# Feed-forward products of a two-block network in 2x2 blocks, with seven products in place of eight

## The chip, the cores and the metric

The kernel runs on one core of a Trainium2 chip. The metric is the device time of one launch in microseconds (us). Every engine of the core works through its own queue of instructions: TensorE (PE) for matrix products, VectorE (DVE), ScalarE (ACT) and GpSimd (POOL) for what is done to their results, and the queue of SyncE (SP) for transfers.

## The reference

A sequence of 512 tokens with 1024 features goes through two blocks, all in float32. The first has two layers, the second one. Each layer is a mixer (attention of several kinds, or RWKV, S5 and gated linear attention), an attention over a memory, and a feed-forward part, so that there are three feed-forward parts. Their inner width is 2816, which is 22 tiles of 128 features. Those of the first block (layers 0 and 1) and of the second are:

```python
def swiglu(h, w_gate_up, w_down):
    g, u = jnp.split(h @ w_gate_up, 2, axis=-1)
    return (jax.nn.silu(g) * u) @ w_down

def conv_ffn(h, w_up, conv_w, conv_b, w_down):
    u = h @ w_up
    u = lax.conv_general_dilated(u, ...) + conv_b      # over 3 tokens, per feature
    gate, val = jnp.split(u, 2, axis=-1)
    return (jax.nn.silu(gate) * val) @ w_down
```

`h` is the RMS norm of `x`, and the result is added to `x`.

## The kernel before

Features lie on the partitions and the 512 tokens along them, so that `x` is eight tiles of 128x512. Float32 values are multiplied as two float32r parts, a high part (ACT, `split` L246 or L310) and a low part, the value less its high part (DVE, `lo` L243, or L312 for weights). `mm3` (L276 to 282) makes three matrix products of each pair: high by high, high by low, low by high. The product of both low parts is left out.

Weights come through `load_split` (L306): a transfer of a chunk of 128x512 to `wraw` (7 buffers), then `wh` and `wl` (5 buffers each). `proj_g` (L316) takes a tile of 128 output features at a time, accumulates over the input tiles in one bank of PSUM of 128x512, and calls `emit` on the bank. Its moving operand is always the whole 512 tokens.

A feed-forward part (`First.ffn` L1166, `Second.ffn` L2342) has two halves of 11 inner tiles. In each, the up stage makes a gate tile and a value tile per inner tile (48 matrix products with eight input tiles). DVE takes the gate out of PSUM times 1/rms, ACT applies the silu, POOL scales once more by 1/rms (L1180), DVE multiplies with the value tile and the result is split. The down stage then makes eight output tiles from these 11 (33 products each), and DVE adds each to `x` (L671). After the second half's sums, `normed` splits `x` times the next gain, and POOL adds up the squares (L446). The second block's part has the convolution on DVE and ACT in the place of the silu's simple chain.

Other work is woven in: jobs are generators, and `fill(us)` runs about so many microseconds of them. In the second feed-forward part one job is there, `s5_make_g`, which computes the tables of S5 on DVE and POOL (L1947 to L2031). Scratch tiles come from pools by stream, which `room` sizes (`z` and a letter). The order of instructions on each engine is set when the program is built, by a list scheduler of the tile framework which goes by the order of the program, by what is ready in its own account of time, and by free buffers. At run time each engine keeps to that order.

Of the kernel before, what the change touches and what calls it, by code (L numbers as in the profile page):

```python
# [10 lines left out]
F32 = mybir.dt.float32  # L11
F32R = mybir.dt.float32r
AF = mybir.ActivationFunctionType
ALU = mybir.AluOpType
# [10 lines left out]
KEEP = {"x": 8, "xs": 16, "acc": 2}  # L25
NRAW = 7
NW = 5
# [14 lines left out]
def chunked(w, cw):  # L42
    """[K, M] -> [M/cw, 128, K/128, cw]: one contiguous run per partition and chunk."""
    k, m = w.shape
    return np.ascontiguousarray(w.reshape(k // 128, 128, m // cw, cw).transpose(2, 1, 0, 3))


def tiled(w, n=2):
    """[K, M] -> [M/(128 n), n, 128, K/128, 128]: groups of n tiles of features."""
    c = chunked(w, 128)  # L50
    return c.reshape(-1, n, *c.shape[1:])


def col(v):
# [15 lines left out]
def rope_tables(ang):  # L70
    """cos, and sin with the sign of the first half, [2 * dim/2, tokens]."""
# [45 lines left out]
def layouts(x, mem, g_mix, w_in_ab, g_qa, g_ka, sink_b, w_out_ab, w_in_cd, g_cq, g_ckv, w_uq, w_ukv,  # L117
# [27 lines left out]
    o["w_gu"] = np.stack([tiled(w.reshape(D, 2 * FF)) for w in gu])  # L145
    o["w_dn"] = np.stack([np.stack([tiled(w_down[i][h * FF // 2 : (h + 1) * FF // 2], 1) for h in range(2)]) for i in range(2)])
# [9 lines left out]
class Kit:  # L156
    """The pools, the constants and the steps that the parts share."""
# [24 lines left out]
    def load(self, name, tag=None, src=None):  # L182
        """An input [128, n], for good (under a tag of its own) or as scratch."""
# [27 lines left out]
    def share(self, roles):  # L211
        """Where the roles take their banks: in turns from each of some pools."""
# [10 lines left out]
    def f(self, n=S, dt=F32, stream=None):  # L223
        """Scratch of [128, n] float32."""
        self.n += 1
        tag = self.streams[self.stream if stream is None else stream]
        return self.z.tile([128, S], dt, tag=tag, name=f"z{tag}_{self.n}", bufs=self.sizes[tag])[:, :n]

    def r(self, n=S, stream=None):
        """Scratch of [128, n] float32r."""  # L230
        return self.f(n, F32R, stream)

    def keep(self, tag, dt=F32):
        """A tile that outlives its part of the program."""
        return self.t([128, S], tag, KEEP[tag], dt)

    def u(self, n=S, stream=None):
        """A split tile [128, n]: two float32r parts."""
        return self.r(n, stream), self.r(n, stream)

# [8 lines left out]
    def split_heads(self, src, tiles, c=None):  # L249
        """The parts of four heads a tile, each head's high beside its low part, for values."""  # L250
# [8 lines left out]
    def split_scaled(self, src, c, hi, lo):  # L259
        """The parts of src times a value per partition."""  # L260
# [4 lines left out]
    def weights(self, src, keep=False):  # L265
        """A chunk [128, kt, cw] of weights from DRAM, split: the parts [128, cw] by kt."""
# [9 lines left out]
    def mm3(self, out, a, b, start, stop, **kw):  # L276
        """out += a.T @ b of split operands; the product of both low parts is below float32's last bit."""
# [6 lines left out]
    def tiles(self, w, step):  # L284
        """The parts of weights by tile of features: of split chunks, or from DRAM, [tiles, 128, kt, m]."""
# [16 lines left out]
    def by(self, *engines):  # L302
        """The engines that take, in turns, the weights' low parts."""
# [11 lines left out]
    def proj_g(self, w, xs, emit, step=128):  # L315
        """Features on partitions: out[i] = W[:, tile i].T @ x."""  # L316
# [9 lines left out]

    def proj_late(self, groups, last):
        """Products of several groups (weights, operands but the last, emit), which wait for it, last(),
        only at their end: three groups of 256 features at a time."""
# [17 lines left out]
    def proj_tok_g(self, w, xs, blocks, emit):  # L347
        """Tokens on partitions: out[b] = x[:, block b].T @ W."""
# [46 lines left out]
    def fill(self, us, own=1.0):  # L395
        """About us microseconds of jobs, in their order as far as they are ready."""
# [15 lines left out]
    def ended(self, O, t):  # L412
        """O[t], once the job that leaves it there has ended."""
# [2071 lines left out]
```

## Time and profile before

| what | us |
|---|---|
| median of 3 runs | 2789.03 (2788.32 to 2790.2) |
| span of the profiled execution | 2782.0 |
| PE, DVE, ACT, POOL busy in it | 2675.9, 1599.8, 1186.2, 517.4 |
| first feed-forward part | about 345 to 704 |
| second feed-forward part | about 1072 to 1470 |
| third feed-forward part | about 2368 to 2740 |

The span is from the first to the last instruction of the profiled execution. The runs are timed from outside, without a profile, and lie 7 us above it. Matrix products are pipelined and their ends are modelled, so their pace is read from one start to the next.

### The profile page before, as it was taken

How to read it: one execution, taken by the hardware profiler on the slowest of the kernel's cores; microseconds unless marked ns; L12 is line 12 of the kernel's file. 1: busy time of each engine (PE TensorE's matmuls, PEld its weight loads, DVE VectorE, ACT ScalarE, POOL GpSimd, SP SyncE). 2: the span in 40 equal slices, each digit the busy share in tenths (PEclk: the TensorE clock that was granted, in tenths of full speed). 3: DMA queues.
4: the chain of work that ended last, by engine and by line, in shares of the span. 5: the costliest groups of instructions: out<-in, count | busy, mean ns of one | idle time of the engine just before them, and what ended most of it. 6: DMA issues, size and time to landing. Idle time of an engine off the chain costs nothing.

```text
span 2782.0 us, 37160 instructions
## 1 busy us (share of the span) xinstructions
PE 2675.9 (96%) x13432; PEld 2152.4 (77%) x13432; DVE 1599.8 (58%) x3076; ACT 1186.2 (43%) x2208; POOL 517.4 (19%) x439
## 2 busy tenths in 40 slices
PE   8999999999999999899999889899999999999998
PEld 6668878888776787678887777687878788888886
DVE  4676654344357967973445567535443556675673
ACT  4566543233345765332334331425223445543442
POOL 5224121011211131250112331112131300100001
PEclk8999999999999999999999989699999999999999
DMA  4112223323322131333433344312211433233332
GB/s 151 35 42 77 72 84 93 101 95 95 110 78 74 49 103 56 109 121 114 142 96 131 113 163 116 99 61 62 81 54 61 124 117 102 83 96 95 99 95 68
DMA packets 172520, 258.51 MB, mean 93 GB/s; under 512 B 42528, under 2 KB 60832, under 8 KB 172320
## 3 DMA queue, kind: packets, MB, share of 16 engines
q1 hardware_dynamic: 172336, 256.13, 29.7%
q8 instruction: 106, 1.74, 0.3%
q14 instruction: 78, 0.64, 0.1%
HBM read 234.04 MB, written 22.15 MB: 92 GB/s over the span
## 4 chain that ended last, share of the span: by engine, by line
PE 54%; DVE 6%; issue 6%; POOL 2%; ACT 1%; DMA 0%; SPq 0%; POOLq 0%; DVEq 0%; ACTq 0%
PE ps_mm L280 14%; PE ps_mm L282 14%; PE ps_mm L281 14%; PE ps_ch L591 1%; DVE wl L312 1%; PE ps_si L2128 1%; POOL rs L466 1%; PE ps_tr L620 1%; PE ps_ch L1537 1%; PE ps_si L2124 0%; PE ps_si L607 0%; PE ps_ch L1610 0%; PE ps_ch L508 0%; PE ps_ch L1611 0%; PE ps_ch L1468 0%
## 5 line engine op out<-in xcount | busy, mean ns | idle before, releaser
L310 ACT CAST wh<-wraw 128x512 fp32r<-128x512 f32 (+1 forms) x777 | 474.5, 614 | 935.4 <-PE ps_mm L281 657.1
L312 DVE TENSOR_TENSOR wl<-wraw,wh 128x512 fp32r<-128x512 f32 (+1 forms) x691 | 484.3, 704 | 359.3 <-ACT wh L310 350.1
L280 PE MATMUL ps_mm<-xs,wh 128*128 128x512 f32 x1544 | 624.2, 404 | 6.2 <-ACT wh L310 5.7
L282 PE MATMUL ps_mm<-xs,wl 128*128 128x512 f32 x1544 | 612.8, 397 | 8.2 <-DVE wl L312 6.7
L281 PE MATMUL ps_mm<-xs,wh 128*128 128x512 f32 x1544 | 614.1, 398 | 0.5 <-DVE xs L262 0.3
L280 PEld LDWEIGHTS ps_mm<-xs,wh 128*128 128x128 f32 x1544 | 293.9, 190 | 77.0 <-issue 9.1
L282 PEld LDWEIGHTS ps_mm<-xs,wl 128*128 128x128 f32 x1544 | 293.7, 190 | 75.9 <-DVE wl L312 8.5
L281 PEld LDWEIGHTS ps_mm<-xs,wh 128*128 128x128 f32 x1544 | 293.8, 190 | 63.3 <-DVE xs L262 4.5
L446 POOL TENSOR_TENSOR acc<-acc,za 128x512 f32<-128x512 f32 x59 | 82.2, 1393 | 732.1 <-ACT za L442 730.4
L280 PE MATMUL ps_mm<-za,wh 128*128 128x512 f32 x460 | 183.5, 399 | 5.6 <-ACT za L246 5.0
L282 PE MATMUL ps_mm<-za,wl 128*128 128x512 f32 x460 | 182.7, 398 | 1.3 <-DVE wl L312 1.3
L281 PE MATMUL ps_mm<-za,wh 128*128 128x512 f32 x460 | 181.3, 394 | 0.1
L312 POOL TENSOR_TENSOR wl<-wraw,wh 128x512 fp32r<-128x512 f32 x86 | 113.4, 1327 | 345.5 <-ACT wh L310 283.8
L1180 POOL TENSOR_TENSOR za<-za,za 128x512 f32<-128x512 f32 x44 | 58.3, 1325 | 508.5 <-ACT za L1179 508.5
L280 PEld LDWEIGHTS ps_mm<-za,wh 128*128 128x128 f32 x460 | 87.9, 191 | 25.0 <-ACT za L246 6.2
L282 PEld LDWEIGHTS ps_mm<-za,wl 128*128 128x128 f32 x460 | 87.8, 191 | 22.0 <-DVE wl L312 1.8
L280 PE MATMUL ps_mm<-zb,wh 128*128 128x512 f32 (+1 forms) x284 | 100.3, 353 | 4.6 <-ACT zb L246 4.1
L281 PEld LDWEIGHTS ps_mm<-za,wh 128*128 128x128 f32 x460 | 87.7, 191 | 20.7 <-DVE za L243 1.0
L281 PE MATMUL ps_mm<-zb,wh 128*128 128x512 f32 (+1 forms) x284 | 98.6, 347 | 0.0
L243 DVE TENSOR_TENSOR za<-ps_tr,za 128x512 fp32r<-128x512 f32 (+3 forms) x152 | 84.3, 558 | 24.6 <-ACT za L246 23.5
L282 PE MATMUL ps_mm<-zb,wl 128*128 128x512 f32 (+1 forms) x284 | 98.3, 346 | 0.0
L466 POOL TENSOR_TENSOR rs<-sm,neghalf 128x4 f32<-128x4 f32 (+2 forms) x32 | 44.8, 1399 | 279.4 <-DVE sm L465 273.0
(592 smaller groups left out, 5013.3 us busy)
## 6 DMA issues: line engine op xcount, KB each, us to landing
wraw<-w_gu SPq DMA_DIRECT2D x176, 256.0 KB, 2.6
wraw<-w_dn SPq DMA_DIRECT2D x96, 256.0 KB, 2.6
wraw<-w_up SPq DMA_DIRECT2D x88, 256.0 KB, 2.6
wraw<-w_gate SPq DMA_DIRECT2D x48, 256.0 KB, 2.6
wraw<-w_dn SPq DMA_DIRECT2D x48, 192.0 KB, 2.3
dram<-za SPq DMA_DIRECT2D x26, 256.0 KB, 2.2
zc<-dram SPq DMA_DIRECT2D x26, 256.0 KB, 5.0
wraw<-w_cd SPq DMA_DIRECT2D x24, 256.0 KB, 2.6
```

What stands on the lines that cost most here:

```text
L243: self.nc.vector.tensor_tensor(lo, src, hi.bitcast(F32), op=ALU.subtract)
L280: mm(out, ah, bh, start=start, stop=False, **kw)
L281: mm(out, ah, bl, start=False, stop=False, **kw)
L282: mm(out, al, bh, start=False, stop=stop, **kw)
L310: self.nc.scalar.copy(hl[0], raw)
L312: eng.tensor_tensor(hl[1], raw, hl[0].bitcast(F32), op=ALU.subtract)
L446: self.nc.gpsimd.tensor_tensor(self.acc[0], self.acc[0], sq, op=ALU.add)
L466: self.nc.gpsimd.tensor_tensor(r, ms, self.neghalf[:, :n], op=ALU.pow)
L591: self.kit.nc.tensor.matmul(p, a[:, b * 128 : b * 128 + 128], c[:, k0:k1], start=i == 0, stop=i == len(self.qk) - 1)
L620: kit.nc.tensor.transpose(tr[:, i * 128 : i * 128 + 128], self.e[b][:, c : c + n], kit.ident)
L1180: nc.gpsimd.tensor_tensor(a, a, st["rb"], op=ALU.mult)
L1537: mm(p[:, i * 256 : i * 256 + 256], blk(st["ka"], e, 2 * g + i), st["ar"][2 * g + i][rows_], start=True, stop=True)
```

## The change

Two output tiles and an even number of input tiles are taken as 2x2 blocks: the weights as a11, a12, a21, a22 (output tile by even or odd input tiles), the moving operand as b11, b12, b21, b22 (even or odd input tiles by the first or last 256 tokens). The eight products of blocks become seven, after Strassen in Winograd's form. `blocks` loads the four chunks of weights, makes four sums of them on POOL and splits seven operands. `forms` makes of two moving tiles the four differences (POOL, or DVE for the last pair) and splits them. `seven` makes the products with 256 moving columns, in banks `x`, `y`, `z`, and continues to accumulate in `x` and `z` after `take` has read them.

This is used for all three down stages (`seven_added`, where each of seven results is added to a half of an `x` tile by DVE) and for the up stage of the first feed-forward part (`up_seven`). The up stages of the second and third keep `proj_g`. The inner tiles are taken in three parts of 4, 4 and 3 pairs in place of two halves of 11 tiles, and one more inner tile is made up before each down stage. The fill after each inner tile is 3.0 for 1.5 us. Memory is divided anew: `wraw` 9 buffers, weights 6, a pool `xt` of 12 tiles that forms, attention's parts and S5's jobs share, 28 tiles `m` for forms of the inner tiles, 5 tiles `s` for sums; the scratch of the mixers is smaller. The diff's other lines take away comments and docstrings.

```diff
-NRAW = 7
-NW = 5
+KEEP = {"x": 8, "xs": 16, "xt": 12, "acc": 2}
+NRAW = 9
+NW = 6
+L, R = slice(0, S // 2), slice(S // 2, S)
+PARTS = 4, 4, 3
...
+    def forms(self, f0, f1, tiles, eng=None):
+        nc = self.nc
+        sub = (eng or nc.gpsimd).tensor_tensor
+        ta, tb = self.f(), self.f()
+        sub(ta[:, L], f0[:, R], f0[:, L], op=ALU.subtract)
+        sub(ta[:, R], f1[:, R], f0[:, R], op=ALU.subtract)
+        sub(tb[:, L], f1[:, R], ta[:, L], op=ALU.subtract)
+        sub(tb[:, R], f1[:, L], tb[:, L], op=ALU.subtract)
+        one = next(tiles)
+        out = {"b11": (one[:, L], one[:, R])}
+        self.split(f0[:, L], *out["b11"])
+        for z, a, b in ((f1, "b21", "b22"), (ta, "t1", "t3"), (tb, "t2", "t4")):
+            hl = next(tiles), next(tiles)
+            self.split(z, *hl)
+            out[a], out[b] = ([y[:, h] for y in hl] for h in (L, R))
+        return out
...
+    def blocks(self, w):
...
+        def both(z):
+            hl = [self.t([128, CW], t, NW, F32R)[:, : n * 128] for t in ("wh", "wl")]
+            self.split(z, *hl)
+            return hl
+        def sum_(x, y, op):
+            z = self.f(n * 128, tag="s")
+            nc.gpsimd.tensor_tensor(z, x, y, op=op)
+            return z
+        yield both(a11)
+        yield both(a12)
+        s1 = sum_(a21, a22, ALU.add)
+        s2 = sum_(s1, a11, ALU.subtract)
+        yield both(s2)
+        yield both(s1)
+        yield both(sum_(a11, a21, ALU.subtract))
+        yield both(sum_(a12, s2, ALU.subtract))
+        yield both(a22)
+    def seven(self, w, xf, take):
...
+        x = self.bank()[:, L]
+        product(x, "b11", True)
+        take("p1", x)
...
+        y = self.bank()[:, L]
+        product(y, "b21", True)
+        take("p2", y)
...
+        product(x, "t2", False)
+        take("u2", x)
...
+        z = self.bank()[:, L]
+        product(z, "t1", True)
+        take("p5", z)
...
+        product(x, "t3", False)
+        take("u3", x)
...
+        product(z, "b22", False)
+        take("p35", z)
...
+        product(x, "t4", False)
+        take("c21", x)
+    def seven_added(self, w, xf, first, second):
+        to = dict(p1=(first, L), p2=(first, L), u2=(first, R), p5=(second, R), u3=(second, R), p35=(first, R), c21=(second, L))
+        def take(step, p):
+            z, h = to[step]
+            self.nc.vector.tensor_tensor(z[:, h], p, z[:, h], op=ALU.add)
+        return self.seven(w, xf, take)
...
+        for at, n in parts:
+            end = min(at + 2 * n + 1, 2 * tiles)
+            while c < end:
+                self.run(up(c, mid(c == 2 * tiles - 1)))
+                self.fill(3.0)
+                c += 1
+            i = parts.index((at, n))
+            for m in range(DT // 2):
+                self.run(self.seven_added(w_dn[i][m], pairs[at // 2 : at // 2 + n], x[2 * m], x[2 * m + 1]))
+                if i == len(parts) - 1:
+                    left(2 * m)
+                    left(2 * m + 1)
...
+            def take(step, p):
+                if step in ("p1", "u2", "p5"):
+                    z = {"p1": a[:, L], "u2": a[:, R], "p5": u[:, R]}[step]
+                    nc.scalar.copy(z, p)
+                elif step in ("p2", "u3", "p35"):
+                    z = {"p2": a[:, L], "u3": u[:, R], "p35": a[:, R]}[step]
+                    nc.vector.tensor_tensor(z, p, z, op=ALU.add)
+                if step == "p35":
+                    nc.vector.tensor_tensor(a, a, rb(), op=ALU.mult)
+                    act(a)
+                    nc.vector.tensor_tensor(u[:, R], u[:, R], a[:, R], op=ALU.mult)
+                elif step == "c21":
+                    nc.vector.tensor_tensor(u[:, L], p, a[:, L], op=ALU.mult)
+                    mid(u)
...
-    kit.room("aaaa", a=50)
+    kit.room("aaaa", a=12, m=28, s=5)
     f.ffn(0, f.g_mix[1])
...
-    kit.room("abbb", a=31, b=50-31)
+    kit.room("axxx", a=12, m=28, s=5)
...
     f.ffn(1, take)
```

The memory attention before the first feed-forward part gives its result through `add_forms`, which makes the forms of `x` times the gain in place of a split.

## Rows read from the trace of the kernel before

**Rows 1.** The page: span, and busy time and count of each engine.
```profile
span 2782.0 us, 37160 instructions
...
PE 2675.9 (96%) x13432; PEld 2152.4 (77%) x13432; DVE 1599.8 (58%) x3076; ACT 1186.2 (43%) x2208; POOL 517.4 (19%) x439
```
**Rows 2.** Windows: length, busy PE, PEld, DVE, ACT, POOL; clock, DMA share, GB/s.
```profile
461.00:523.00 62.00, 62.00 (x273) 51.07 (x272) 23.34 (x37) 18.02 (x30) 3.88 (x3) 1.00 0.33 93
523.00:640.00 117.00, 117.00 (x516) 96.65 (x515) 47.57 (x72) 36.82 (x61) 10.33 (x8) 1.00 0.31 98
...
1072.00:1470.00 398.00, 376.72 (x1749) 307.09 (x1748) 235.13 (x602) 140.87 (x238) 92.66 (x107) 0.97 0.35 111
2368.00:2740.00 372.00, 371.39 (x1649) 306.00 (x1648) 240.04 (x356) 170.02 (x262) 13.53 (x10) 1.00 0.31 94
```
**Rows 3.** Timeline in the first up stage: start us, duration us, instruction.
```profile
457.39 0.39 PE L282 MATMUL ps_ch<-xs,wl 128*128 128x512 f32 x1
...
457.62 0.39 PE L280 MATMUL ps_ch<-xs,wh 128*128 128x512 f32 x1
```
**Rows 4.** Timeline, products of 256 columns in the second block's memory attention.
```profile
2239.51 0.28 PE L280 MATMUL ps_mm<-zb,wh 128*128 128x256 f32 x1
2239.51 0.19 PEld L281 LDWEIGHTS ps_mm<-zb,wh 128*128 128x128 f32 x1
...
2239.98 0.28 PE L281 MATMUL ps_mm<-zb,wh 128*128 128x256 f32 x1
```
**Rows 5.** Groups by form: count, busy us, mean ns, idle before.
```profile
L312 DVE TENSOR_TENSOR wl<-wraw,wh 128x512 fp32r<-128x512 f32 x108 | 74.3, 688 | 91.2 <-ACT wh L310 91.1
L310 ACT CAST wh<-wraw 128x512 fp32r<-128x512 f32 x108 | 67.3, 623 | 178.3 <-PE ps_ch L281 60.6 <-PE ps_mm L281 59.3 <-PE ps_si L281 56.6
L1180 POOL TENSOR_TENSOR za<-za,za 128x512 f32<-128x512 f32 x22 | 28.4, 1292 | 262.8 <-ACT za L1179 262.8
...
L2246 POOL TENSOR_TENSOR zb<-zb,zb 128x256 f32<-128x256 f32 x7 | 5.6, 804 | 6.0 <-ACT zb L2245 6.0
```
**Rows 6.** Timeline of POOL and DVE where DVE starts second.
```profile
160.73 1.30 POOL L312 TENSOR_TENSOR wl<-wraw,wh 128x512 fp32r<-128x512 f32 x1 [5.36 <-ACT wh L310]
161.21 1.37 DVE L243 TENSOR_TENSOR zb<-zb,zb 128x512 fp32r<-128x512 f32 x1 [1.01 <-ACT zb L246]
```
**Rows 7.** Timeline of DVE and POOL where POOL starts second.
```profile
994.60 0.69 DVE L312 TENSOR_TENSOR wl<-wraw,wh 128x512 fp32r<-128x512 f32 x1
994.86 1.58 POOL L312 TENSOR_TENSOR wl<-wraw,wh 128x512 fp32r<-128x512 f32 x1 [2.38 <-ACT wh L310]
995.59 0.42 DVE L1083 TENSOR_TENSOR zb<-ps_mm,zb 128x256 f32<-128x256 f32 x1 [0.29 <-PE ps_mm L282]
```
**Rows 8.** Timeline of POOL and DVE near 1250 us.
```profile
1249.31 4.94 POOL L1975 TENSOR_TENSOR zb<-zb,zb 128x144 f32<-128x144 f32 x1 [2.59 <-DVE zb L1978]
...
1250.69 2.82 DVE L312 TENSOR_TENSOR wl<-wraw,wh 128x512 fp32r<-128x512 f32 x5
```
**Rows 9.** Timeline of POOL and DVE, alternating, in S5's job.
```profile
1242.09 0.50 POOL L1975 TENSOR_TENSOR zb<-zb,zb 128x144 f32<-128x144 f32 x1
1242.21 0.54 DVE L1972 TENSOR_TENSOR zb<-zb,zb 128x144 f32<-128x144 f32 x1
1242.56 0.50 POOL L1977 TENSOR_TENSOR zb<-zb,zb 128x144 f32<-128x144 f32 x1
```
**Rows 10.** Timeline at the first part's start: a low part, and who waits for it.
```profile
367.17 1.76 DVE L312 TENSOR_TENSOR wl<-wraw,wh 128x512 fp32r<-128x512 f32 x1
...
368.98 0.50 PE L282 MATMUL ps_mm<-xs,wl 128*128 128x512 f32 x1 [2.87 <-DVE wl L312]
```
**Rows 11.** Timeline of PE in the second part, where S5's job comes.
```profile
1180.65 1.94 PE L2029 MATMUL ps_ch<-ident,zb 128*128 128x128 f32 x8 [11.42 <-DVE zb L2022]
...
1183.24 0.63 PE L282 MATMUL ps_mm<-xs,wl 128*128 128x512 f32 x1
1183.67 0.63 PE L280 MATMUL ps_mm<-xs,wh 128*128 128x512 f32 x1
```

More of the change, by code (lines that the diff above doesn't have):

```diff
@@ L51, in tiled, with halved, parted, parts_of @@
     return c.reshape(-1, n, *c.shape[1:])
+def halved(w):
+    t = w.reshape(w.shape[0] // 128, 128, -1)
+    return np.concatenate([t[0::2], t[1::2]]).reshape(w.shape)
+def parted(w):
+    out, at = [], 0
+    for n in PARTS:
+        out.append(tiled(halved(w[at * 256 : (at + n) * 256])).reshape(-1))
+        at += n
+    return np.concatenate(out)
+def parts_of(src):
+    out, at = [], 0
+    for n in PARTS:
+        size = D * n * 256
+        out.append(src[at : at + size].rearrange("(c j p k m) -> c j p k m", j=2, p=128, k=2 * n, m=128))
+        at += size
+    return out
 def col(v):
@@ new lines, in blocks @@
+    def blocks(self, w):
+        nc, n = self.nc, w.shape[2] // 2
+        raw = {}
+        for j in range(2):
+            for h in range(2):
+                z = raw[j, h] = self.t([128, CW], "wraw", NRAW)[:, : n * 128]
+                nc.sync.dma_start(z.rearrange("p (k m) -> p k m", m=128), w[j, :, h * n : h * n + n, :])
+        (a11, a12, a21, a22) = raw[0, 0], raw[0, 1], raw[1, 0], raw[1, 1]
+        def both(z):
[15 more added lines that the diff above has]
+        yield both(a22)
@@ new lines, in seven, with product @@
+    def seven(self, w, xf, take):
+        a = self.blocks(w)
+        def product(p, form, start):
+            hl = next(a)
+            for k, x in enumerate(xf):
+                self.mm3(p, [z[:, k * 128 : k * 128 + 128] for z in hl], x[form], start and k == 0, k == len(xf) - 1, skip_group_check=True)
+        us = len(xf) * 0.35
+        x = self.bank()[:, L]
+        product(x, "b11", True)
+        take("p1", x)
+        yield us
+        y = self.bank()[:, L]
+        product(y, "b21", True)
+        take("p2", y)
+        yield us
+        product(x, "t2", False)
+        take("u2", x)
+        yield us
+        z = self.bank()[:, L]
+        product(z, "t1", True)
+        take("p5", z)
+        yield us
+        product(x, "t3", False)
+        take("u3", x)
+        yield us
+        product(z, "b22", False)
+        take("p35", z)
+        yield us
+        product(x, "t4", False)
+        take("c21", x)
+        yield 0
@@ L423, in flush, with ffn_parts, mid, f @@
             self.fill(1.0)
+    def ffn_parts(self, up, w_dn, x, left):
+        parts, tiles, mids = [], sum(PARTS), []
+        for n in PARTS:
+            parts.append((2 * sum(PARTS[: len(parts)]), n))
+        pairs = []
+        held = (self.f(S, F32R, tag="m") for _ in range(7 * tiles))
+        def mid(last):
+            def f(z):
+                mids.append(z)
+                if len(mids) % 2 == 0:
+                    pairs.append(self.forms(*mids[-2:], held, self.nc.vector if last else None))
+            return f
+        c = 0
+        for at, n in parts:
[10 more added lines that the diff above has]
+                    left(2 * m + 1)
     def normed(self, m, x, g, squares=True):
@@ L436, in normed, with normed_forms @@
             self.squares(m, x)
+    def normed_forms(self, m, x, g):
+        f = self.f()
+        self.nc.scalar.activation(f, x, AF.Copy, scale=g)
+        if m == 0:
+            self.xs, self.held = [], chain((self.keep("xs", F32R) for _ in range(16)), (self.keep("xt", F32R) for _ in range(12)))
+        if m % 2:
+            self.xs.append(self.forms(self.even, f, self.held, self.nc.vector if m == DT - 1 else None))
+        else:
+            self.even = f
+        self.squares(m, x)
     def squares(self, m, x, direct=1):
@@ L685, in rotate, with parts @@
         return a
-    def parts(self, a):
-        hl = self.kit.u()
+    def parts(self, a, held=True):
+        hl = [self.kit.keep("xt", F32R) for _ in range(2)] if held else self.kit.u()
         self.kit.split(a, *hl)
@@ L1169, in ffn, with rb @@
         st = {}
-        for half in range(2):
-            mid = []
-            for c in range(FT // 2):
-                def gate(j, p):
-                    if "rb" not in st:
-                        st["rb"] = kit.spread(kit.rstd(), 4)
-                    if j == 0:
-                        a = kit.f()
-                        nc.vector.tensor_tensor(a, p, st["rb"], op=ALU.mult)
-                        nc.scalar.activation(a, a, AF.Silu)
-                        nc.gpsimd.tensor_tensor(a, a, st["rb"], op=ALU.mult)
-                        st["a"] = a
-                    else:
-                        nc.vector.tensor_tensor(st["a"], p, st["a"], op=ALU.mult)
-                        hl = kit.u()
-                        kit.split(st["a"], *hl)
-                        mid.append(hl)
-                kit.run(kit.proj_g(I["w_gu"][i, half * (FT // 2) + c], xs, gate))
-                kit.fill(1.5)
-            for m in range(DT):
-                kit.run(kit.proj_g(I["w_dn"][i, half, m], mid, lambda j, p: self.down(m, p, g if half else None)))
+        def rb():
+            if "rb" not in st:
+                st["rb"] = kit.spread(kit.rstd(), 4)
+            return st["rb"]
```

95 lines of the change are left out of this document (55 added, 40 removed).

## The prediction

> **What bounds the kernel now.** I read the page first: its span is 2782.0 us, in which PE is busy 96%, DVE 58%, ACT 43% and POOL 19% [rows 1]. PE is the bound on average, but the change lies in three stages only, so the windows come next. In the first feed-forward part, in a down stage (461 to 523 us) and an up stage (523 to 640), PE is busy for the whole stretch at full clock; DVE has some 40% of each and POOL less than a tenth [rows 2]. The second loses 21 us of 398 and the third almost none [rows 2].
>
> A busy PE is not PE at its peak, so the pace is read from starts. Products of 512 columns start 0.227 us apart, 457.39 and 457.62 for two of the first up stage [rows 3]. The 273 products between 461 and 523 us come to the same: 62/273 = 0.227 us [rows 2]. One part has 22 x 2 x 8 x 3 = 1056 products up and 8 x 22 x 3 = 528 down, at 0.2275 us 240.2 and 120.1 us. These stages are bound by PE alone, and only here are fewer products worth their time.
>
> Is a product of 256 columns worth half? The memory attention has such products with weights of 128x128: of five in a row the first starts at 2239.51 and the last at 2239.98, a weight load beside each [rows 4]. Four steps in 0.47 us are 0.117 us.
>
> **PE's part.** Two tiles of output features against 2n tiles of inner ones needed 12n products of 512 columns and now need 7 x 3n = 21n of 256. With n = 4 that is 10.92 us before and 84 x 0.117 = 9.83 us after; with n = 3 it is 8.19 and 7.37 us. The first part's up stage has 22 sets with n = 4: 216.2 us for 240.2, a gain of 24.0. Each down stage has eight sets of n = 4 and four of n = 3: 108.1 for 120.1, a gain of 12.0, three times. PE gains 60 us at most. That holds where the other engines keep pace with 9.83 us a set.
>
> **What the others must do for it.** A set took four splits of weights (ACT for the high part, DVE for the low) and now takes seven, and POOL makes four sums of 128x512 besides. Prices from [rows 5]: a cast 0.62 us, a low part on DVE 0.69, a POOL operation of 128x512 1.29 and of 128x256 0.80. An ACT copy out of PSUM of half the width I count as a cast, 0.62 at most. A PSUM operation of 128x256 on DVE takes 0.42 [rows 7].
>
> Up stage with seven products, per set: ACT 7 x 0.62 + 3 x 0.62 + 0.62 for the silu + half of 3.5 casts = 7.9 us. POOL: four sums and the gate's scale, 5 x 1.29, and half of four 256-column differences, 1.6, together 8.05. DVE: seven low parts, one product of 512 and one of 256, half of 3.5 low parts for the forms, all with both inputs in SBUF, 7 x 0.69 + 0.69 + 0.42 + 1.2 = 7.1; and four operations out of PSUM, 1.7. One by one each is below 9.83. The question is whether DVE and POOL can do it at the same time.
>
> The trace says no. At 160.73 POOL begins 1.30 us of work; at 161.21 DVE begins a low part that takes 0.69 elsewhere, and it ends 0.55 us after POOL does, 1.37 us long [rows 6]. The other way: POOL begins at 994.86 under a DVE low part, and ends 1.15 us after it [rows 7]. Five low parts in a row held a small POOL operation for 4.94 us [rows 8]. DVE's operations out of PSUM do not suffer: the one at 995.59 takes 0.42 us and is over 0.43 us before POOL's end [rows 7]. So where both inputs are in SBUF, DVE and POOL take turns, and I count 0.55 us for a DVE turn of 512 columns and 1.15 for POOL's. Where operations of 144 columns alternate, POOL's start 0.47 us apart with DVE's between them, though the two records are 0.50 and 0.54 us long [rows 9]: a record holds some waiting, and a turn is shorter. And PE does wait for it: at 368.98 it has lost 2.87 us to a low part that took 1.76 us [rows 10].
>
> Turns in an up set: POOL 5 x 1.15 + 2 x 0.6 (half of 1.15, and a little) = 6.95; DVE 9.5 x 0.55 + 1.5 x 0.29 = 5.66. That is 12.6 us where PE needs 9.83 and took 10.92 before. Whole records added, without overlap, give 8.05 + 7.1 = 15.1. The Trainium skill, "SBUF — State Buffer", section "SBUF: two separate sides", states it as a rule: a DVE operation with two SBUF inputs and a GpSimd operation lock the same port pair for a whole instruction, and the other blocks; the trace agrees in kind, and by whole instructions the set would take 15.1 us, where the alternating operations show part of the start hidden [rows 9]. I take 13.8, midway, since the queues are in order: DVE stands at an accumulation that PE has not finished, or at a low part whose sum POOL has not made. 22 x 13.8 = 304 us for 240: **+63** (12.6 gives +37, 15.1 gives +92).
>
> **Down sets.** With n = 4 the turns are 4 x 1.15 + 7 x 0.55 = 8.45, under 9.83. But DVE also takes seven PSUM sums of 0.42, in order between the low parts, and four of the seven products continue in a bank whose last value must first be read, with one product of 1.4 us between. Bounds: 9.83 if everything hides; 7 x 0.69 + 7 x 0.42 + 4 x 1.29 = 12.93 if nothing does. I take 10.5, near PE's own figure since about half of the sums can lie under POOL's turns: 24 sets x (10.5 - 10.92) = **-10** (-26 to +48). With n = 3, three quarters of POOL's record are 0.97 and of a low part's 0.52, so the bounds are 7.37 and 7 x 0.52 + 7 x 0.42 + 4 x 0.97 = 10.46; I take 8.5: 12 x 0.3 = **+4** (-10 to +27).
>
> **The smaller edits.** In each last set the next norm comes too: two low parts scaled on DVE and two POOL sums of squares (four at the handover, two and no low parts at the end), which slack hid before: 3.5, 5.8 and 2.3 us of turns per set, 47 us in all over 12 sets if none is hidden, 0 if POOL may run late. **+12**, a quarter, because sums of squares can trail into the next stage. At the first part's start, eight tiles are made into forms: three pairs with 12 differences of 0.80 on POOL beside the squares, where the 2.87 us wait is today. PE's first product needs only the undiffered quarter, so I take **+8** (3 to 15). The last pair of each part is made on DVE: four dependent operations of 0.42 and a split of 1.3, about 3 us, less the products that don't need it: **+6** for three (3 to 12). The S5 job lies in the second part; PE waited 11.42 us for it until 1180.65 [rows 11]. It now gets twice the fill and 12 buffers that it shares, and POOL's and DVE's new work is in its way: **+5** (-10 to +20). The rest (nine raw buffers, six of weights, smaller rooms for attention, weights laid out in another order at equal bytes) I cost at nothing: weight transfers land in stretches where DMA is busy a third of the time [rows 2], and attention takes its keys and queries from a pool of its own for what it gives up; without that cover it would cost a few us, inside the range.
>
> **Sum.** 63 - 10 + 4 + 12 + 8 + 6 + 5 = +88. The profiled execution had a span of 2782; the median of the runs is 2789.0, 7 us around it. 2782 + 88 + 7 = **2877 us**. All lower bounds together give -3 (2786), all upper ones +261 (3050).
>
> **Rivals.**
> 1. *PE stays the bound.* POOL's sums run far enough ahead and the turns fall into gaps: every set takes PE's time, -60, and with the start and the last pairs about 2743. For it: DVE is idle more than half of the time in these stages today and POOL most of it [rows 2], and each alone stays under 9.83 us. Against it: the turns seen [rows 6 to 8], 12.6 us of them a set. It decides if a set's turns stay under 9.83 us, that is, if POOL's turn of 512 columns were 0.69 us instead of 1.15. Chance 0.13, faster.
> 2. *All at the lower bounds*: 12.6 us per up set, down sets at PE's pace, 2786. Chance 0.09, split evenly between faster, same and slower.
> 3. *The down sets are bound by the turns too*: the sums out of PSUM don't fit under POOL's turns and PE waits at each bank it continues in. 24 x 1.3 + 12 x 1.8 = +53 in place of -6, with the last sets' 30: about 2955, at most 3050. Chance 0.15.
> 4. *The clock falls.* If PE waits a quarter of the up stage, its granted clock may drop as it did after the 11 us wait, where products of 512 columns went from 0.23 to 0.43 us apart [rows 11]. A product of 256 would take half of that, a set 84 x 0.215 = 18 us, the stage 397: +157, with the rest about 2970. Against it: the waits here are of a few us at most, and the second part, which lost 21 us to its waits, kept a mean clock of 0.97 [rows 2]. Chance 0.05.
>
> The forecast keeps 0.58, with a range of its own of 2835 to 2930. "Same" means within 0.2%, 5.6 us, about what a measurement of this kernel can tell from no change. Faster 0.13 + 0.03 = 0.16, same 0.03, slower 0.58 + 0.15 + 0.05 + 0.03 = 0.81. The range that leaves out rival 1 and the upper part of rival 3, 0.2 together, is 2775 to 2980.
>
> **What would show it.** Products of 256 columns 0.117 us apart within a product set; the first up stage about 300 us long, with PE waiting before low parts of weights and DVE's low parts at a mean of 1 us or more; POOL busy for over half of that stage; down sets near 10.5 and 8.5 us. The prediction is wrong if low parts stay at 0.69 us beside a busy POOL, if PE shows no waits for them, or if 256-column products start further apart than 0.12 us.

## The result and the profile after

The changed kernel takes 2935.6 us (median of 4 runs, 2934.4 to 2936.4) for 2788.7 (4 runs of the kernel before on the same chip): 1.053 times the time before, 95% interval 1.052 to 1.055. The forecast was 2877 us with 2775 to 2980 around it, so the sign and the range hold; the size is 59 us short, and the time is just above the forecast's own range of 2835 to 2930.

The page of the changed kernel, the lines that answer to [rows 1], and the costliest groups on DVE and POOL that the change made:

```profile
span 2933.4 us, 42837 instructions
...
PE 2694.5 (92%) x15412; PEld 2246.8 (77%) x15412; DVE 2041.2 (70%) x3632; ACT 1325.0 (45%) x2531; POOL 964.8 (33%) x803
...
L272 DVE TENSOR_TENSOR wl<-zs,wh 128x512 fp32r<-128x512 f32 (+1 forms) x232 | 237.6, 1029 | 25.5 <-ACT wh L275 21.8
...
L393 POOL TENSOR_TENSOR zs<-wraw,wraw 128x512 f32<-128x512 f32 (+1 forms) x116 | 152.7, 1317 | 88.8 <-DVE wl L272 44.9
```

PE is still busy for 92% of the span, which would pass for "bound by PE" if one stopped here. But its busy time did not fall at all (2694.5 us for 2675.9), though it has less to do, and the low parts of sums take a mean of 1029 ns (two widths together; 1087 at 128x512 alone) for 688 in [rows 5]. So the windows come next: the first set with its start, the other sets of the first up stretch, a down stage of the first part, the second up stretch (eight sets), and a down stage of the third part. The columns are those of [rows 2].

```profile
374.00:422.00 48.00, 28.37 (x150) 25.07 (x149) 35.57 (x40) 24.18 (x44) 38.68 (x30) 0.68 0.15 45
422.00:531.00 109.00, 85.69 (x627) 83.23 (x626) 88.45 (x117) 48.71 (x99) 66.17 (x53) 0.91 0.26 75
531.00:578.00 47.00, 42.17 (x339) 41.45 (x339) 41.66 (x60) 18.22 (x30) 21.34 (x17) 0.96 0.31 91
578.00:690.00 112.00, 89.82 (x676) 87.58 (x675) 91.81 (x119) 50.62 (x102) 70.28 (x56) 0.92 0.26 76
...
2642.00:2689.00 47.00, 40.92 (x340) 40.05 (x339) 43.46 (x66) 20.13 (x34) 14.48 (x11) 1.00 0.32 92
```

In the second stretch DVE and POOL together are busy for 162 of 112 us, and PE stands for 22 of them; before, it stood for none [rows 2]. Eight sets in 112 us are 14.0 each.

Where the time went, by the first matrix product of each stage to the first of the next, in the profiled executions (good to some 0.2 us):

| stage | before | after | difference |
|---|---|---|---|
| ahead of the first feed-forward part | 362.1 | 374.4 | +12.3 |
| first part: up stage | 247.4 | 334.8 | +87.4 |
| first part: down stage | 120.7 | 135.9 | +15.2 |
| mixer and memory attention after it | 364.7 | 390.4 | +25.7 |
| second part | 399.7 | 403.3 | +3.6 |
| second block's mixer and attention | 908.5 | 902.4 | -6.1 |
| third part | 363.4 | 375.9 | +12.5 |
| rest | 15.5 | 16.3 | +0.8 |

The sum is 151.4, the difference of the spans. Of the +12.3 ahead of the first part some 11 lie in one stretch of half clock near 60 us. It appeared in two other executions of the experiments and was absent from the rest, although the program there is the same in several of them, and layout, with the same memory, reaches the first part at 364.4 us. So I put it down to the execution and not to the change. Whether the changed kernel's other timed runs had it too is not on record; differences between runs below may hold some 10 us of this kind.

One pair of sets shows how PE comes to stand. The timeline of the second up stretch (start, duration, instruction, and in brackets what the engine waited for):

```profile
591.56 1.74 POOL L1351 TENSOR_TENSOR za<-za,za 128x512 f32<-128x512 f32 x1
...
593.33 1.50 DVE L1380 TENSOR_TENSOR za<-za,za 128x256 f32<-128x256 f32 x1 [1.18 <-POOL za L1351]
...
594.75 0.41 DVE L1382 TENSOR_TENSOR za<-ps_mm,za 128x256 f32<-128x256 f32 x1
...
595.20 0.62 ACT L275 CAST zm<-za 128x512 fp32r<-128x512 f32 x1 [3.65 <-DVE za L1382]
...
598.46 0.37 ACT L1373 COPY za<-ps_mm 128x256 f32<-128x256 f32 x1
...
598.88 0.58 PE L309 MATMUL ps_mm<-xs,wh 128*128 128x256 f32 x1 [4.16 <-ACT za L1373]
```

Read it from the end. PE waits 4.16 us for ACT to copy a product out of the bank in which PE is to go on. In ACT's queue the casts of the pair's forms, and of weights, stand ahead of that copy: the first of them waited 3.65 us for DVE, and they keep ACT until 598.46. DVE had stood 1.18 us for POOL's scale, and then its product of 256 columns, 0.41 us where nothing is in the way, took 1.50, under POOL's next operation. PE's waits from 376 to 845 us say how often that is:

```profile
PE ps_mm L309 <- ACT za L1373: 56.0, 27, 4.2
PE ps_mm L309 <- DVE x L449: 13.2, 10, 3.4
```

The trace names ACT, but ACT is the messenger: what is late is the shared work of DVE and POOL, as the runs without it show below.

### The profile page after: what moved, and what is told of

It reads as the page before. It is cut to its first block, busy times and chain, and to the rows that moved or that the text cites. A ratio compares the mean times of both kernels' runs of the same rounds, so it can differ in the third digit from the quotient of the medians.

```text
span 2933.4 us, 42837 instructions
## 1 busy us (share of the span) xinstructions
PE 2694.5 (92%) x15412; PEld 2246.8 (77%) x15412; DVE 2041.2 (70%) x3632; ACT 1325.0 (45%) x2531; POOL 964.8 (33%) x803
## 5 line engine op out<-in xcount | busy, mean ns | idle before, releaser
L309 PE MATMUL ps_mm<-xs,wh 128*128 128x512 f32 (+1 forms) x1614 | 642.0, 398 | 73.1 <-ACT za L1373 56.0
L310 PE MATMUL ps_mm<-xs,wh 128*128 128x512 f32 (+1 forms) x1614 | 628.5, 389 | 5.7 <-DVE xs L291 4.2
L311 PE MATMUL ps_mm<-xs,wl 128*128 128x512 f32 (+1 forms) x1614 | 626.1, 388 | 1.5 <-POOL wl L341 1.5
L339 ACT CAST wh<-wraw 128x512 fp32r<-128x512 f32 x545 | 334.6, 618 | 537.0 <-PE ps_mm L310 411.2
L341 DVE TENSOR_TENSOR wl<-wraw,wh 128x512 fp32r<-128x512 f32 x459 | 339.1, 742 | 140.7 <-ACT wh L339 135.4
L309 PE MATMUL ps_mm<-zm,wh 128*128 128x256 f32 x792 | 228.2, 289 | 44.9 <-DVE x L449 37.8
L272 DVE TENSOR_TENSOR wl<-zs,wh 128x512 fp32r<-128x512 f32 (+1 forms) x232 | 237.6, 1029 | 25.5 <-ACT wh L275 21.8
L310 PE MATMUL ps_mm<-zm,wh 128*128 128x256 f32 x792 | 224.3, 283 | 1.3 <-DVE zm L272 1.1
L311 PE MATMUL ps_mm<-zm,wl 128*128 128x256 f32 x792 | 223.3, 283 | 0.8 <-DVE wl L272 0.8
L309 PEld LDWEIGHTS ps_mm<-zm,wh 128*128 128x128 f32 x792 | 150.9, 191 | 54.3 <-ACT wh L275 20.0
L310 PEld LDWEIGHTS ps_mm<-zm,wh 128*128 128x128 f32 x792 | 151.6, 191 | 2.4 <-DVE zm L272 2.2
L272 DVE TENSOR_TENSOR wl<-wraw,wh 128x512 fp32r<-128x512 f32 (+1 forms) x174 | 148.0, 859 | 3.9 <-ACT wh L275 3.1
L275 ACT CAST wh<-wraw 128x512 fp32r<-128x512 f32 (+1 forms) x174 | 101.8, 594 | 87.7 <-PE ps_mm L310 62.6
```

Of the source, the lines that this page charges most:

```text
L272: self.nc.vector.tensor_tensor(lo, src, hi.bitcast(F32), op=ALU.subtract)
L275: self.nc.scalar.copy(hi, src)
L309: mm(out, ah, bh, start=start, stop=False, **kw)
L310: mm(out, ah, bl, start=False, stop=False, **kw)
L311: mm(out, al, bh, start=False, stop=stop, **kw)
L339: self.nc.scalar.copy(hl[0], raw)
```

## The experiments

**The memory layout alone, and the parts of the change.** Four kernels: the kernel before with the new memory layout only; and the changed kernel with the first up stage in eight products, with the weights' sums on DVE, and without the sums.

```diff
# layout: the kernel before with the new buffers, rooms and the pool xt
-    kit.room("abbb", a=31, b=50-31)
+    kit.room("axxx", a=45)
# up_plain
-        self.kit.ffn_parts(up if i else up_seven, ...
+        self.kit.ffn_parts(up, ...
# sums_dve
-            nc.gpsimd.tensor_tensor(z, x, y, op=op)
+            nc.vector.tensor_tensor(z, x, y, op=op)
# no_sums
-            z = self.f(n * 128, tag="s")
-            nc.gpsimd.tensor_tensor(z, x, y, op=op)
-            return z
+            return x
```

> The kernel before with only the changed memory: pools, buffers of raw and split weights, attention's keys and queries in a pool of 12, smaller scratch; all feed-forward products as before. If the smaller scratch is what lengthens the stages before the first and the second feed-forward part by 14 and 26 us, this runs at about 2825 us, with both stages as long as in the changed kernel. If those stages suffer from something else (the clock, what the feed-forward part leaves behind), it stays within 6 us of 2789.

> The changed kernel with the first up stage in eight products again (256-column forms of x gone), the down stages in seven. If the up stage with seven products costs what the profile of the changed kernel shows, 333 us for 240 and a longer start, this is 85 to 100 us faster than the changed kernel, about 2840 us. If the first part is long for a reason that lies outside its up stage, it stays near 2935 us.

> The changed kernel with the four sums of weights on DVE, none on POOL. Turns: the low parts no longer wait for sums on POOL; DVE has 7.1 + 1.7 + 2.8 = 11.6 us in an up set and 10.5 in a down set of four, so the first part falls from 469 to about 370 us, each set of four down to 10.6, and the whole to about 2820 us. Rival, the hand-over of banks (PE waits for a value to be read before it continues in that bank): DVE, which reads most of them, gets more work and the time is the same or longer, 2935 us or more.

> The changed kernel without the four sums of weights: the first of each sum's two operands is split and used in its place, so that all products, splits and reads remain and POOL's work for weights is gone. Turns: up sets near 10.5 us and down sets at 9.9 and 7.6 us, the whole at about 2780 us. Rival, the hand-over of banks: nothing of it changes, and the time stays above 2900 us.

Measured: layout 2797.7 us (ratio 1.003, 1.001 to 1.005); up_plain 2835.5 (1.014, 1.011 to 1.018); sums_dve 2859.3 (1.024, 1.022 to 1.027); no_sums 2805.2, one run. up_plain came out as expected; layout lies between the two figures of its expectation, and sums_dve and no_sums are 39 and 25 us slower than theirs, though far below their rival's. So the first up stage in seven products costs 100 us against eight products with all else changed; the sums cost 130 us, the most by far (122 of them within the three feed-forward parts, by the profiled executions); and moving them to DVE, the busier of the two engines, gives 76 of the 130 back. Without the sums the second up stretch is short, its clock stays full, and PE is busy for 95% of it:

```profile
522.00:607.00 85.00, 80.81 (x673) 79.99 (x672) 74.28 (x118) 51.70 (x102) 24.21 (x22) 1.00 0.31 99
```

That is 10.6 us a set, still above PE's own 9.83, and hardly less than the 10.92 of eight products. With the sums on DVE a set takes 11.9.

The layout by itself looks nearly harmless in the total, but not by stage: the mixer and memory attention ahead of the second part took 389.3 us for 364.7, and the second part 390.9 for 399.7. So nearly all of the changed kernel's +25.7 there comes from memory, which the prediction had at nothing. Windows over the later part of that stage, the memory attention in it, the kernel before and then layout:

```profile
876.00:1095.00 219.00, 214.79 (x1143) 172.91 (x1143) 168.35 (x334) 144.40 (x307) 33.70 (x25) 0.99 0.23 67
```

```profile
876.00:1119.00 243.00, 224.43 (x1146) 177.02 (x1147) 217.95 (x605) 149.76 (x321) 40.24 (x36) 0.97 0.22 68
```

PE has the same products, but DVE has 605 instructions for 334. One line of the S5 job, in the kernel before and in layout, says whose they are:

```profile
L1931 DVE TENSOR_TENSOR zb<-zb,zb x7: 172/175/1282, 1160.4 to 1170.8; 128x16 f32<-128x16 f32 x7
```

```profile
L1933 DVE TENSOR_TENSOR xt<-xt,xt x7: 165/177/1283, 1029.3 to 1048.7; 128x16 f32<-128x16 f32 x7
```

The job's scratch now comes from the pool `xt`, which lasts for the whole program. It no longer waits for the room that opens with the second part, and the scheduler puts it 130 us earlier, into stages where DVE is already busy for 77% of the time.

**Is it contention, or a late operand?** no_sums takes away three things at once: POOL's work beside DVE's, the chain from raw weights over a sum to the split, and the wait for it. Two kernels keep POOL busy and take the chain away.

```diff
# sums_unused: the same four operations, of raw weights; the splits take raw weights
             nc.gpsimd.tensor_tensor(z, x, y, op=op)
-            return z
+            return x
# sums_memset
-            z = self.f(n * 128, tag="s")
-            nc.gpsimd.tensor_tensor(z, x, y, op=op)
-            return z
+            for _ in range(2):
+                z = self.f(n * 128, tag="s")
+                nc.gpsimd.memset(z, 0.0)
+            return x
```

> GpSimd makes the same four sums per set, of raw operands, but nothing reads them: the splits take the raw operands (the products are therefore those of other weights). What remains of the sums is GpSimd's work beside VectorE's and the time that the raw buffers are held. Theory of turns: nearly all of the 130 us that leaving the sums out gave back is contention, so this takes 2890 to 2935 us, with up sets of 12.5 us or more and low parts at a mean near 0.9 us. Rival, latency (PE waits for a chain raw, sum, high part, low part whose operand comes late): about 2805 to 2830 us, as without the sums. In between would give each its share.

> In place of each sum GpSimd writes two constant tiles of 128x512 (0.52 us each in the profile, so about 1.05 us for a sum's 1.28), and the splits take raw operands (products of other weights). GpSimd is busy about as long as with the sums, but reads nothing from SBUF. If what VectorE loses is lost to GpSimd's reads of two tiles, this is like the kernel without sums, 2800 to 2815 us, with low parts of weights at 0.70 us. Rival: any GpSimd work takes VectorE's turns, or GpSimd's queue itself is late: 2850 us or more, low parts above 0.85 us.

Measured: sums_unused 2935.0 us (ratio 1.053, 1.050 to 1.055), the changed kernel's own time. Its four runs spread from 2925.8 to 2943.3. Nothing reads its sums, so on the whole a late operand costs nothing, and POOL's work by itself makes up the 130 us. By stage the two kernels are not quite alike: down sets of four pairs are 0.5 us shorter than in the changed kernel, those of three as much longer. A third way, weights that land late because the sums hold their raw buffers, does not show either: from 374 to 845 us ACT's splits, which take the raw weights first, wait for no transfer here, and for 5 us in all in the changed kernel; only POOL's unused sums wait for transfers. What is left is contention between the two engines, and the order of POOL's queue, which the next two runs tell of. Its groups between 580 and 690 us, most of which is the second up stretch:

```profile
L272 DVE TENSOR_TENSOR wl<-wraw,wh 128x512 fp32r<-128x512 f32 x57 | 63.9, 1122 | 9.3 <-ACT wh L275 8.6
...
L393 POOL TENSOR_TENSOR zs<-wraw,wraw 128x512 f32<-128x512 f32 x32 | 53.0, 1685 | 18.9 <-DMA wraw<-w_dn 12.0 <-DMA wraw<-w_gu 6.8
```

Low parts at 1122 ns and sums at 1685, for 688 and 1292 undisturbed [rows 5]: each holds the other.

sums_memset took 2842.0 us (1.018, 1.016 to 1.020), between the two expectations, and the reason is where the writes went. They wait for nothing, so the scheduler heaped them up: none in the second up stretch, where the sets are those of no_sums, and 103 between 420 and 480 us. That stretch tells the two causes apart. Its groups on DVE and POOL:

```profile
L272 DVE TENSOR_TENSOR wl<-wraw,wh 128x512 fp32r<-128x512 f32 x33 | 24.7, 755 | 5.1 <-ACT wh L275 4.8
...
L1381 DVE TENSOR_TENSOR za<-za,za 128x256 f32<-128x256 f32 x4 | 1.7, 422 | 6.5 <-POOL za L1352 6.5
...
L394 POOL MEMSET zs<- 128x512 f32 x103 | 48.7, 523 | 0.0
```

POOL is busy for 59.5 of the 60 us, and DVE's low parts take 755 ns: a POOL operation that only writes does not hold DVE. (In the same window of no_sums they take 855; more of the pairs' differences fall into it.) Yet the sets here take 13.0 us for the 10.6 of no_sums, because the gate's scale stands in POOL's queue behind the writes and DVE waits for it. A full queue costs too, by its order, and not by the ports. The Trainium skill, "SBUF — State Buffer", section "SBUF: two separate sides", limits the lock of a DVE operation with two SBUF inputs to a GpSimd operation that reads SBUF; these rows bear it out.

**The scale.** The wait of 1.18 us in the timeline above is for the gate's scale on POOL.

```diff
-            nc.gpsimd.tensor_tensor(a, a, rb(), op=ALU.mult)
+            nc.vector.tensor_tensor(a, a, rb(), op=ALU.mult)
```

> The changed kernel, with the gate's scale by 1/rms in the first and second feed-forward parts moved from GpSimd to VectorE. In the changed kernel VectorE stands 1.2 us a set for this scale, in order, and then waits again for GpSimd's next sum. Theory (turns, and each engine in its order): one of GpSimd's five turns of 512 columns goes, VectorE gets one of its own, and the wait goes: up sets of 12.7 to 13.4 us in place of 14.0, 15 to 30 us less, 2905 to 2920 us. Rival: the sums alone set the pace, and the scale was hidden behind them: 2930 us or more.

Measured: 2906.4 us (1.042, 1.040 to 1.044), 29 us less than the changed kernel; eight sets of the second stretch take 106.9 us, 13.4 each for 14.0. As the theory said: DVE does one more operation per set, at 693 ns, and the set is shorter. The first part gains 15 us in its up stage and 9 in its down stages, and the rest is of the size by which executions differ; the second part, which has the edit too but no such sets in its up stage, gains nothing (403.9 us for 403.3).

```profile
L1351 DVE TENSOR_TENSOR za<-za,za 128x512 f32<-128x512 f32 x7 | 4.8, 693 | 0.7
```

**The memory again.** Which part of the layout costs the 25 us? (Like layout, both kernels also carry one more difference of the changed kernel, `dynamic_dma_scratch_size=1024` where the program is set up. No run tests it by itself.)

```diff
# s5_late: layout, with a room of the job's own
-    kit.room("axxx", a=45)
+    kit.room("abbb", a=29, b=16)
# bufs_only: the kernel before with
-NRAW = 7
-NW = 5
+NRAW = 9
+NW = 6
```

> The kernel before with the new memory layout, but the S5 job's scratch comes from a room that opens with the second feed-forward part (29 + 16 tiles) and not from the pool of 12 that lasts for the whole program. Theory: with the common pool the scheduler puts 238 of the job's VectorE operations into the mixer and the memory attention ahead of that part, where VectorE is already busy for three quarters of the time, and this makes these stages 25 us longer and the part after them 9 us shorter. Then here those stages take about 365 us in place of 389, the part about 400, the whole 2782 to 2792 us. Rival: the smaller rooms for attention cost the 25 us: the stages stay at 385 to 390 us and the whole is 2800 us or more.

> The kernel before with 9 raw and 6 weight buffers and nothing else changed. Theory: of the 25 us that the mixer and the memory attention ahead of the second feed-forward part lost with the new memory layout, 13 came from the S5 job's earlier place (given back in the part after) and about 7 of the rest from these buffer counts, by another order of transfers and splits: those stages take about 372 us for 364.7, the whole 2790 to 2800. Rival: the counts are harmless and the smaller rooms took it: 365 us and 2785 to 2791 us.

Measured: s5_late 2796.1 us (1.002, 1.000 to 1.004), bufs_only 2787.3 (1.001, 0.9995 to 1.003). By stage, mixer with memory attention and then the second part: before 364.7 and 399.7, bufs_only 368.1 and 404.9, s5_late 376.4 and 404.3, layout 389.3 and 390.9. So the stage lands halfway between theory and rival. The job's early place costs 12.9 us in the one stage and gives 13.4 back in the other, nothing on the whole: the theory had the place right and the net cost wrong. The buffer counts cost 3 and 5 us by stage, though the runs' median, in the rival's range, says nothing measurable. The smaller rooms cost another 8. These last are differences of a few us between single profiled executions, and not more than hints.

**A version that keeps what pays.** With the sums on DVE, the down sets of four pairs are the ones that are shorter than plain ones (10.1 to 10.4 us where no S5 work is beside them, for 10.92). `mixed` takes the kernel before and does the first eight pairs of inner tiles of the first and the third part's down stages in seven products, sums on DVE; all up stages, the last six inner tiles and the second part are plain.

```diff
-            nc.gpsimd.tensor_tensor(z, x, y, op=op)
+            nc.vector.tensor_tensor(z, x, y, op=op)
...
-                if len(mids) % 2 == 0:
+                if len(mids) > 16:
+                    hl = self.u()
+                    self.split(z, *hl)
+                    plain.append(hl)
+                elif len(mids) % 2 == 0:
# mixed_small: mixed with the buffer counts of before
-NRAW = 9
-NW = 6
+NRAW = 7
+NW = 5
```

> Memory rooms and the second feed-forward part as in the kernel before; in the first and the third part the up stage in eight products, the first two down stages (four pairs of inner tiles) with seven products and their sums on VectorE, the last six inner tiles with plain products. From the runs so far a down stage of four pairs with sums on VectorE takes 40.2 and 41.5 us for 43.7 plain, four of them -11 us; the pairs' differences on GpSimd and a wait before each down stage may cost 1 us each. Forecast 2779 us (2772 to 2790), ratio 0.996. Rival: the differences and extra splits delay the up stages beside them, or the stage starts wait, and the gain is gone: 2788 us or more.

> As mixed, but with 7 raw and 5 weight buffers as in the kernel before, so that its mixers and its second feed-forward part are the kernel before's in order too. Theory: in mixed the first and third parts gained 9 and 5 us, and the larger buffer counts took back some 7 us in the mixers and 7 in the second part, through another order. Then this takes 2772 to 2780 us, ratio 0.993 to 0.997. Rival: a set with seven products needs more than seven raw buffers to have its next four chunks in time; then the down sets with seven products are 11 us or longer in place of 10.05, and the whole is 2785 us or more.

Measured: mixed 2784.0 us (0.998, 0.996 to 0.9996); mixed_small 2775.6 (0.996, 0.9945 to 0.9975, against 2785.7 of the kernel before on that chip). mixed_small is faster than both kernels, by 10 us or 0.4%. Its windows of the two down stages of the first part, the up stretch between them, and a down stage of the third part:

```profile
466.00:506.00 40.00, 39.80 (x337) 39.59 (x336) 35.47 (x67) 17.69 (x29) 1.12 (x1) 1.00 0.30 101
506.00:593.00 87.00, 87.00 (x387) 72.08 (x386) 50.46 (x71) 32.85 (x55) 27.74 (x23) 1.00 0.30 100
593.00:633.00 40.00, 40.00 (x339) 39.82 (x338) 35.56 (x67) 17.96 (x29) 0.00 (x0) 1.00 0.31 100
2498.00:2540.00 42.00, 39.94 (x336) 39.54 (x335) 39.44 (x75) 19.33 (x33) 1.05 (x1) 1.00 0.29 96
```

The first down stages are at PE's own pace, four sets in 40 us for 43.7 plain, with DVE busy for 89% of the time. In the third part DVE is at 94%, and PE stands for 2 of 42 us. Seven raw buffers are enough for sets of four chunks. That it beats mixed by the mixers and the second part, as was expected, fits these stages (367.1 and 403.6 us for 371.7 and 406.8), but the two ran on different chips and the differences are small.

## Why the prediction was right in sign and short in size

First, two readings to put right. The times of the feed-forward parts ahead of the prediction, and the windows that it calls a down and an up stage [rows 2], lie too early: by the inputs of the matrix products the parts run from 362 to 730, 1095 to 1495 and 2403 to 2766 us, and the first part's first down stage and second up stage from 490 to 550 and from there to 670. What was read from them holds, since PE is busy throughout these two as well, DVE for 35 and 42% of them and POOL for none and 12%. And the 4.94 us of [rows 8] are not held by five low parts alone: six small DVE operations run ahead of them in it, and the low parts take 2.82 us.

**PE's part** stood. Products of 256 columns start 0.12 us apart in the changed kernel, and with nothing in the way a set is at PE's pace (the two 40 us windows above). That the two other engines would not keep pace stood as well.

**The up sets**, the largest term, were sized right: 13.8 us forecast, 14.2 measured as the mean of the 19 steps between sets inside the three stretches (from one set's last multiplication on DVE to the next's), so +71 for +63. The mechanism is the one named, and sums_unused and no_sums show that it is the cause. The turn of a low part stood too: in the third part's down stage DVE's starts second, and ends 0.54 us after POOL does, for the estimate of 0.55 from [rows 6].

```profile
2658.66 1.29 POOL L393 TENSOR_TENSOR zs<-wraw,zs 128x512 f32<-128x512 f32 x1 [0.68 <-POOL zs L393]
...
2658.78 1.71 DVE L272 TENSOR_TENSOR wl<-zs,wh 128x512 fp32r<-128x512 f32 x1
```

By the rule of whole instructions (the Trainium skill, "SBUF — State Buffer", section "SBUF: two separate sides") a set would have been 15.1 us by the prediction's estimate. The 14.2 lies between that and the 12.6 of turns.

Two things were missing from the working. A set's cost is uneven: the set after the end of a pair takes 15 to 16 us and the others 13, because ACT, in its order, holds the copy that PE needs behind the pair's casts. And that the sum came so near is in part luck. The working left the clock to rival 4, but after each of the long waits PE's next products start 0.21 us apart, at the lower of the clock's two levels, and not 0.12:

```profile
599.47 0.41 PE L311 MATMUL ps_mm<-xs,wl 128*128 128x256 f32 x1
599.68 0.41 PE L309 MATMUL ps_mm<-xs,wh 128*128 128x256 f32 x1
...
602.75 0.28 PE L310 MATMUL ps_si<-xt,wh 128*128 128x256 f32 x1
602.87 0.28 PE L311 MATMUL ps_si<-xs,wl 128*128 128x256 f32 x1
```

In the second stretch 76 of 672 steps are of that kind, with the granted clock at 0.92, and cost 7 us, 0.9 a set. Without them its sets would be 13.1 us for 14.0, an estimate, below the forecast 13.8.

**The start of the first part** is a step that failed: +8 was forecast because "PE's first product needs only the undiffered quarter". The first set ends, again by DVE's last multiplication, 47.8 us after the first product, 33.6 more than a set's 14.2; before, the start cost 7.6 us over the pace (127.5 us for the first eleven inner tiles, 119.9 for the second). That is +26, of which some 10 come back where later sets reach into the down stages. The first product does start early. Then PE stands again and again for what comes one after another behind POOL: differences, and the squares that `rstd` needs, which the scale of the first set needs; POOL's first sums come behind them.

```profile
383.44 0.58 PE L309 MATMUL ps_mm<-xs,wh 128*128 128x256 f32 x1 [3.31 <-ACT xs L275]
...
391.12 0.59 PE L627 MATMUL ps_tr<-ones,acc 128*128 128x1 f32 x2 [4.65 <-POOL acc L615]
...
400.94 0.58 PE L309 MATMUL ps_mm<-xs,wh 128*128 128x256 f32 x1 [4.31 <-ACT wh L275]
```

While it stands its clock goes down to the lower of its levels, as rival 4 had it, though not in the whole stage: the granted clock is 0.50 between 390 and 400 us, and 0.68 over the 48 us of the first set. In the second stretch it is 0.92.

```profile
380.00:390.00 10.00, 2.49 (x8) 1.50 (x6) 5.86 (x7) 6.45 (x13) 9.74 (x10) 0.52 0.00 1
390.00:400.00 10.00, 5.43 (x22) 4.84 (x22) 4.99 (x10) 2.82 (x6) 4.73 (x4) 0.50 0.01 2
```

**The down sets** were sized too low. With four pairs they take 11.4 us (six stages, 272.9 us for 24 sets) for a forecast 10.5: +11 where -10 stood. With three pairs, norms included, 10.5 us (125.8 for 12), +27 where +4 and +12 stood. This is rival 3 in part: the turns bind here too. The step at fault is "about half of the sums can lie under POOL's turns". They do lie there, but POOL's sums hold the low parts behind them: the two rows from 2658.66 us, with 1.71 us for a low part, repeat through the set, and 5 to 9 low parts of each such stage take 1.6 us or more. Without the sums sets of four pairs take 10.1 us, at PE's pace; with them on DVE 10.1 in the first part. Sets of three pairs take 9.1 to 9.9 even without sums, for PE's 7.37: with the next norm's work DVE is busy for 96% of such a stage, here the second part's without sums.

```profile
1483.00:1522.00 39.00, 32.86 (x252) 31.16 (x251) 37.44 (x66) 26.35 (x51) 15.53 (x10) 0.97 0.31 95
```

That points to DVE as the bound by itself there; no run tests it.

**Memory at nothing** was wrong: +25.7 in the mixer and memory attention, and layout shows that nearly all of it comes from memory. The stated cover, attention's keys in a pool of its own, was no cover: the pool is also the S5 job's, which frees it from its room. The term for the job, +5, had looked at the second part only; there the stall of 11.42 us [rows 11] did go. A job has to be priced in every stage into which its buffers let it go.

**The last pairs** (+6) came out as sized. In the last down stage of each part PE waits for the splits of the last pair (`zm`), for 2.0, 1.1 and 2.3 us; these 5.4 us are within the sets of three pairs above.

**The 7 us** that the sum adds to the span are no cost of timing. In every run with its own span on record the time lies only about 2 us above it (2935.2 for 2933.4); the profiled execution of the kernel before was a faster one than the median.

## What to carry to other kernels

Fewer products are a gain only if the operands they need cost less than the time saved, on an engine that has it to give. Before moving arithmetic to GpSimd, count POOL's operations that read SBUF and DVE's with both inputs there as one queue: here the work was cheaper on the busier VectorE than on an idle-looking GpSimd. And a buffer pool is part of the schedule: a job whose scratch comes free earlier runs earlier, in a stage that nobody meant to change.

## What the runs showed of the hardware that was not expected

- A POOL operation that only writes SBUF left DVE's low parts at 755 ns with POOL busy for 59.5 of 60 us; beside sums that read two tiles they took 1122 ns on average (sums_unused, 580 to 690 us), and up to 1.8 us in the changed kernel.
- DVE's operations with one input in PSUM kept their 0.41 us beside POOL's sums throughout; only those with both inputs in SBUF suffered. That is why the sums' cost shows in the splits of the weights, and not in the operations that read PSUM.
- The Trainium skill, "Perfetto Trace Analysis", section "Optimizing Scalar/DVE Operations", says that moving operations between VectorE and GpSimd might not help, since they share a port. Here it is stronger: moving the sums away from GpSimd to VectorE gained 76 us, and the scale 29.
